# Second product of the MLP: 16 of its 22 K tiles as seven half-block products, with sums of weights made by adding DMAs

## The chip, the cores and the metric

One core of a Trainium2 chip runs the whole program. The metric is the time of one execution on the device, in microseconds; the median of three runs is given, and one more execution was recorded by the hardware profiler. The names of the engines are those of the profile: PE (TensorE, matrix products), PEld (its weight loads), DVE (VectorE), ACT (ScalarE), POOL (GpSimd), SP (SyncE, which here only issues DMAs).

## What is computed

One layer of a decoder: token mixers, a projection, and a gated MLP, all in float32. The part that matters here is the end:

```
h = rmsnorm(x, ln_ffn_g)                          # x: 512 tokens x 1024
a, u = split(h @ w_ffn_in)                        # 1024 -> 2 x 2816
a = causal_dwconv(a, conv_w, conv_b)
x = x + (silu(a) * u) @ w_ffn_out                 # 2816 -> 1024
```

## The kernel before

Everything is cut into tiles of 128: 4 blocks of tokens, 8 tiles of the model's width, 22 tiles of the MLP's width. A product of float32 data is done as three matmuls in the type float32r: an operand x is split into a high half (a cast on ACT, `wh`) and a low half (x minus the high half, on DVE, `wl`), and high x high, high x low and low x high are added up in PSUM (`mm3`). Activations get the same split when they are made.

Weights arrive in units of up to 1 MB on SP's queue (`load`; tile `raw`, four buffers). A unit is used in chunks. For each chunk `split_steps` casts and subtracts (`wh` has four buffers, `wl` three), and a function of the chunk issues the matmuls. The main loop at the end of the program goes over the chunks and asks for the splits of the current one and the next two. PE's instructions stand in program order (`order`); so do POOL's DMAs (`pool`); on ACT and DVE a scheduler sets the order among what is independent.

The first product (`ffn_group`) already uses seven products instead of eight half-block products (the Strassen form with Winograd's order of sums). Sums of activations are made on DVE. Sums of weights are made in place, in the tile `raw`: as soon as a chunk has been split, a DMA from POOL's queue adds another 512 KB block of the weights from HBM onto it (`then`, `accum_op=ALU.add`), and the next chunk that uses the tile splits the sum.

The second product is plain. The gated activations lie in `gT` (22 tiles of 128 x 512 tokens). `fo_split` makes their halves, two tiles ahead. All eight PSUM banks are held through the product: 4 token blocks x 2 halves of the 1024 columns. One chunk is one K tile (128 x 1024 weights): 8 x 3 matmuls of 512 columns, with the activations as the stationary operand and the weights moving. The last three K tiles (`TAIL`) are taken bank by bank, so that a finished bank is added to the residual `x1` on DVE (L794) and stored on SP's queue (L795) while PE works on the next. The residual was put into HBM (`spill`) before the first product and is loaded back when the second begins.

## Time and profile before

| | us |
|---|---|
| median of three runs (803.85 to 804.54) | 803.97 |
| the profiled execution, its own time | 803.51 |
| its span, first to last instruction | 801.7 |
| PE busy in the span | 789.6 |
| DVE busy | 524.2 |
| ACT busy | 371.5 |
| POOL busy | 161.1 |

An execution takes a little longer than its span. PE's busy time is the sum of modelled, overlapping matmuls, so its steps are better read from the starts of matmuls than from their lengths. The granted clock of PE is 0.998 of full speed over the span, which is the upper of its two levels, 2.4 GHz.

### The profile page before, as it was taken

Reading aid. Unit: us, or ns where it says so; the run is one execution under the profiler, and the core shown is the slowest. Engines: PE = TensorE matmul, PEld = TensorE weight load, DVE = VectorE, ACT = ScalarE, POOL = GpSimd, SP = SyncE. Lnnn points to the kernel's source line nnn. Section 1 sums busy time; section 2 is a strip of 40 time slices with the busy share of each in tenths; the row PEclk is TensorE's granted clock in tenths of the full one; section 3 lists DMA queues with packets and bytes.
Section 4 is the critical chain, followed back from the end, with each engine's and each line's share of the span. In section 5 each row is a group of like instructions: output and inputs, shape, how many; then the busy total and the mean of one; then the engine's idle time right before and its main releaser. Section 6 shows DMA issues by size and latency. Waiting matters only on the chain.

```text
span 801.7 us, 11534 instructions
## 1 busy us (share of the span) xinstructions
PE 789.6 (98%) x4550; PEld 693.9 (87%) x4550; DVE 524.2 (65%) x805; ACT 371.5 (46%) x566; POOL 161.1 (20%) x221
## 2 busy tenths in 40 slices
PE   8999999999999999999999999999999999999997
PEld 8888888878878888888888999999999999788886
DVE  5777656764989883546744767867777778623323
ACT  6663333547644542533432755555555665423210
POOL 1510010004767740000010131212222320000000
PEclk9999999999999999999999999999999999999999
DMA  9513132231212113232593399789999995432002
GB/s 326 159 52 105 55 104 75 83 106 53 76 63 72 54 54 103 81 106 83 197 272 105 83 162 204 146 161 185 180 185 184 170 222 181 149 105 74 32 1 106
DMA packets 74888, 98.49 MB, mean 123 GB/s; under 512 B 3644, under 2 KB 60578, under 8 KB 74834
## 3 DMA queue, kind: packets, MB, share of 16 engines
q1 hardware_dynamic: 51490, 74.57, 28.0%
q0 software_dynamic: 23232, 23.07, 19.2%
q8 instruction: 36, 0.59, 0.3%
q14 instruction: 18, 0.15, 0.1%
q10 hardware_dynamic: 112, 0.10, 0.0%
HBM read 93.54 MB, written 4.19 MB: 122 GB/s over the span
## 4 chain that ended last, share of the span: by engine, by line
PE 83%; DVE 7%; DMA 3%; POOL 2%; ACT 2%; issue 2%; SPq 0%; ACTq 0%; POOLq 0%; DVEq 0%
PE ps L84 81%; DMA raw<-in_w_ffn_in_dram 2%; PE ps L107 2%; DVE wl L271 1%; DVE stQ L887 1%; POOL stQ L892 1%; DMA raw<-in_w_in_dram 1%; ACT acth L319 1%; DVE t2a L705 1%; DVE t2a L704 1%; DVE scr L930 0%; DVE gT L707 0%; DVE stK L873 0%; ACT wh L270 0%; ACT t4a L331 0%
## 5 line engine op out<-in xcount | busy, mean ns | idle before, releaser
L271 DVE TENSOR_TENSOR wl<-raw,wh 128x1024 fp32r<-128x1024 f32 (+1 forms) x152 | 186.7, 1230 | 117.3 <-PE ps L84 59.7
L270 ACT CAST wh<-raw 128x1024 fp32r<-128x1024 f32 (+1 forms) x150 | 157.1, 1048 | 208.7 <-PE ps L84 164.1
L84 PE MATMUL ps<-wh,acth 128*128 128x512 f32 (+1 forms) x352 | 131.9, 385 | 0.5 <-DVE wh L268 0.5
L84 PE MATMUL ps<-s,wh 128*128 128x256 f32 x704 | 129.3, 285 | 2.5 <-ACT gT L689 2.5
L84 PE MATMUL ps<-wl,acth 128*128 128x512 f32 (+1 forms) x352 | 130.3, 381 | 0.8 <-DVE wl L271 0.8
L84 PE MATMUL ps<-wh,actl 128*128 128x512 f32 (+1 forms) x352 | 130.3, 381 | 0.0
L84 PEld LDWEIGHTS ps<-s,wh 128*128 128x128 f32 x704 | 110.2, 192 | 2.7 <-ACT gT L689 2.7
L718 POOL DMA_DIRECT2D raw<-in_w_ffn_in_dram x44 | 56.7, 1289 | 254.9 <-DVE wl L271 132.6
L84 PE MATMUL ps<-s,wl 128*128 128x256 f32 x352 | 100.3, 285 | 0.0
L84 PE MATMUL ps<-a,wh 128*128 128x256 f32 x528 | 96.3, 283 | 0.0
L84 PEld LDWEIGHTS ps<-a,wh 128*128 128x128 f32 x528 | 81.8, 190 | 0.1
L84 PE MATMUL ps<-acth,wh 128*128 128x512 f32 x192 | 79.4, 413 | 0.0
L84 PEld LDWEIGHTS ps<-wh,acth 128*128 128x128 f32 x352 | 64.7, 188 | 13.4 <-issue 1.5
L84 PEld LDWEIGHTS ps<-wl,acth 128*128 128x128 f32 x352 | 64.7, 188 | 13.3 <-DVE wl L271 1.4
L84 PEld LDWEIGHTS ps<-wh,actl 128*128 128x128 f32 x352 | 64.7, 188 | 12.8
L84 PE MATMUL ps<-acth,wl 128*128 128x512 f32 x192 | 75.1, 391 | 0.0
L84 PE MATMUL ps<-actl,wh 128*128 128x512 f32 x192 | 74.9, 390 | 0.0
L84 PE MATMUL ps<-a,wl 128*128 128x256 f32 x264 | 74.7, 283 | 0.0
L84 PEld LDWEIGHTS ps<-s,wl 128*128 128x128 f32 x352 | 67.5, 192 | 0.0
L84 PEld LDWEIGHTS ps<-a,wl 128*128 128x128 f32 x264 | 50.1, 190 | 0.0
L892 POOL TENSOR_TENSOR stQ<-stQ,qk 128x128 f32<-128x128 f32 (+2 forms) x80 | 46.3, 605 | 10.4 <-ACT stQ L90 8.7
L84 PEld LDWEIGHTS ps<-acth,wl 128*128 128x128 f32 x192 | 36.0, 188 | 7.9
(233 smaller groups left out, 1229.1 us busy)
## 6 DMA issues: line engine op xcount, KB each, us to landing
raw<-in_w_in_dram SPq DMA_DIRECT2D x22, 1024.0 KB
raw<-in_w_ffn_in_dram POOLq DMA_DIRECT2D x44, 512.0 KB, 6.5
raw<-in_w_ffn_in_dram SPq DMA_DIRECT2D x22, 512.0 KB
raw<-in_w_ffn_out_dram SPq DMA_DIRECT2D x11, 1024.0 KB
b<-in_w_ffn_in_dram SPq DMA_DIRECT2D x11, 512.0 KB
raw<-in_w_branch_b_dram SPq DMA_DIRECT2D x4, 1024.0 KB
raw<-in_w_out_dram SPq DMA_DIRECT2D x4, 1024.0 KB
x<-in_x_dram SPq DMA_DIRECT2D x4, 512.0 KB
```

What stands on the lines that cost most here:

```text
L84: order(nc.tensor.matmul(ps, lhsT, rhs, start=start, stop=stop, skip_group_check=more))
L107: order(nc.tensor.transpose(ps, src, idn))
L270: nc.scalar.copy(h[:, k], src[:, k])
L271: nc.vector.tensor_sub(l[:, k], src[:, k], h[:, k].bitcast(F32))
L319: nc.scalar.mul(hT[0][:, k, tok], ps, g)
L704: nc.vector.scalar_tensor_tensor(t, A[:, c, 1:S + 1], col(1), t, ALU.mult, ALU.add)
L705: nc.vector.scalar_tensor_tensor(t, A[:, c, 0:S], col(0), t, ALU.mult, ALU.add)
L718: pool(nc.gpsimd.dma_start(loaded[u][:, half[a], :], chain[a], accum_op=ALU.add))
L887: nc.vector.tensor_tensor(v[:, :, :, c], Bg[:, hs, :, t], r.broadcast_to([P, 2, P // (per * L), (per - 1 - j) * L]), ALU.subtract)
L892: nc.gpsimd.tensor_tensor(v[:, :, :, c], v[:, :, :, c], qg[:, hs, :, t], ALU.mult)
```

## The change

The first six K tiles of the second product stay plain; when they are done, the eight banks are added into `x1` in SBUF. The other sixteen tiles become two halves of eight K tiles, the tokens two halves of 256, the columns two halves of 512, and the product is done as seven half-block products in the order of `FSEQ`. One of them is 8 K tiles x 2 token blocks x 3 = 48 matmuls of 512 columns, in four chunks of two K tiles. `fo_part` makes the activations' operand of the product that follows, with sums on DVE; `fo_evac` adds each finished product into `x1`, or keeps it in `F["v"]`; a12 goes on adding in the banks of a11, and s4 in those of s1. Three blocks of weights are loaded (2 MB each: for a11, a12 and s4); the weights of the other four products arise in those tiles by sixteen adding DMAs of 512 KB. The last three chunks of a22 are taken bank by bank. Units are fetched two ahead instead of three from the start of the first product on.

The diff, without its empty lines:

```diff
--- before.py
+++ after.py
@@ -249,9 +249,13 @@
         if i not in split and i < len(chunks):
             run(split_steps(i))
 
+    def ahead(i):
+        return 2 if i < 2 or i >= n_o else 3
     def split_steps(i):
         u, sl, shape, _ = chunks[i]
-        for uu in range(u, u + 3 if i > 1 else 2):
+        for uu in range(u, u + ahead(i)):
             load(uu)
         n = shape[0] * shape[1]
         src = sl() if callable(sl) else loaded[u][:, sl[0], sl[1]]
@@ -743,62 +747,157 @@
         groups[g](a)
     n_fi = len(chunks)
 
-    fo_act = []
+    FP, FH = 6, 8
+    fo, fo_act = {}, []
 
     def fo_split(j):
         if j < 2:
             H, L = tmp([P, S], "gh", F32R), tmp([P, S], "gl", F32R)
         else:
             if j == 2:
-                fo_act.extend(act_pair("act"))
-            H, L = (t[:, j % KT, :] for t in fo_act)
+                fo_act.extend(v3(slot(n, F32R), 4) for n in ("foh", "fol"))
+            H, L = (t[:, j - 2, :] for t in fo_act)
         nc.scalar.copy(H, gT(j))
         nc.vector.tensor_sub(L, gT(j), H.bitcast(F32))
         return H, L
 
-    TAIL = 3
-    fo = {}
-    def fo_mm(i, j, b, half, wh, wl, H, L):
-        ps = st["fo"][b][half]
-        t, w = slice(b * P, (b + 1) * P), slice(half * 512, (half + 1) * 512)
-        matmul(ps, H[:, t], wh[:, 0, w], start=j == 0, stop=False)
-        matmul(ps, H[:, t], wl[:, 0, w], start=False, stop=False)
-        matmul(ps, L[:, t], wh[:, 0, w], start=False, stop=j == NF - 1)
-    early = {}
     def fo_ready(j):
-        for jj in range(j + 1):
-            if jj < NF and jj not in early and jj not in fo:
-                early[jj] = fo_split(jj)
+        for jj in range(min(j + 1, FP)):
+            if jj not in fo:
+                fo[jj] = fo_split(jj)
+    def x1q(b, half):
+        return x1(b)[:, half * 512:(half + 1) * 512]
 
     def fo_chunk(j):
         def mm(i):
             if j == 0:
                 st["fo"] = [[bank() for _ in range(2)] for _ in range(NB)]
             fo_ready(j + 2)
-            fo[j] = (i, j) + (split[i], early.pop(j))
-            if j < NF - TAIL:
-                for b in range(NB):
-                    for half in range(2):
-                        fo_mm(i, j, b, half, *split[i], *fo[j][3])
-            elif j == NF - 1:
-                for b in range(NB):
-                    for half in range(2):
-                        for jj in range(NF - TAIL, NF):
-                            ii, _, (wh, wl), (H, L) = fo[jj]
-                            fo_mm(ii, jj, b, half, wh, wl, H, L)
-                        w = slice(half * 512, (half + 1) * 512)
-                        o = tmp([P, 512], "t2a")
-                        nc.vector.tensor_tensor(o, st["fo"][b][half], x1(b)[:, w], ALU.add)
-                        nc.sync.dma_start(out[b * P:(b + 1) * P, w], o)
+            if j >= FP - 4:
+                for c in range(FH // 2 * (j - FP + 4) // 4, FH // 2 * (j - FP + 5) // 4):
+                    fo_part("a11", c)
+            (H, L), (wh, wl) = fo[j], split[i]
+            for b in range(NB):
+                t = slice(b * P, (b + 1) * P)
+                for half in range(2):
+                    ps, w = st["fo"][b][half], slice(half * 512, (half + 1) * 512)
+                    mm3(ps, H[:, t], L[:, t], wh[:, 0, w], wl[:, 0, w], j == 0, j == FP - 1)
+                    if j == FP - 1:
+                        nc.vector.tensor_tensor(x1q(b, half), ps, x1q(b, half), ALU.add)
         return mm
 
-    for j in range(0, NF, 2):
+    for j in range(0, FP, 2):
         u = unit([((ALL, ALL), w_fo.rearrange("(k p) c -> p k c", p=P)[:, j:j + 2, :])], (2, D))
         for c in range(2):
             chunk(u, (slice(c, c + 1), slice(0, D)), (1, D), fo_chunk(j + c))
+    FSEQ = ("a11", "a12", "s1", "s2", "s4", "s3", "a22")
+    fop, F = {}, {}
+    def fo_part(a, c):
+        if a not in fop:
+            fop[a] = [v3(slot(f"fo{a}", F32R), FH) for _ in range(2)]
+        (a11, a21), (a12, a22) = ([gT2(FP + half + 2 * c)[:, :, t] for t in (slice(0, 256), slice(256, S))]
+                                  for half in (0, FH))
+        src = {"a11": a11, "a12": a12, "a22": a22, "s2": a21}.get(a)
+        if src is None:
+            src = tmp([P, 2, 256], f"f{a}")
+            if a == "s1":
+                nc.vector.tensor_sub(src, a21, a22)
+                nc.vector.tensor_sub(a21, a11, src)
+            else:
+                nc.vector.tensor_sub(src, a12 if a == "s4" else a22, a21)
+        h, l = (t[:, 2 * c:2 * c + 2, :] for t in fop[a])
+        nc.scalar.copy(h, src)
+        nc.vector.tensor_sub(l, src, h.bitcast(F32))
+    def fo_evac(a, b):
+        ps = F[a][b]
+        lo, hi = b, 2 + b
+        def put(y):
+            nc.sync.dma_start(out[y[0] * P:(y[0] + 1) * P, y[1] * 512:(y[1] + 1) * 512], x1q(*y))
+        def add(y, z, sub=False):
+            nc.vector.tensor_tensor(x1q(*y), x1q(*y), z, ALU.subtract if sub else ALU.add)
+        if a == "a11":
+            if b == 0:
+                F["v"] = tmp([P, 2, 512], "fv")
+            nc.scalar.copy(F["v"][:, b, :], ps)
+            return
+        v = F["v"][:, b, :]
+        if a == "a12":
+            add((lo, 0), ps)
+            put((lo, 0))
+        elif a == "s1":
+            add((hi, 1), ps)
+        elif a == "s2":
+            nc.vector.tensor_sub(v, ps, v)
+            add((lo, 1), v)
+        elif a == "s4":
+            add((lo, 1), ps)
+            put((lo, 1))
+        elif a == "s3":
+            nc.vector.tensor_add(v, ps, v)
+            add((hi, 1), v)
+            put((hi, 1))
+            add((hi, 0), v, True)
+        else:
+            add((hi, 0), ps)
+            put((hi, 0))
+    def fo_mm(a, c):
+        def mm(i):
+            on = {"a12": "a11", "s4": "s1"}.get(a)
+            if c == 0:
+                F[a] = F[on] if on else [bank() for _ in range(2)]
+            n = FSEQ.index(a) + 1
+            if n < len(FSEQ):
+                fo_part(FSEQ[n], c)
+            nc_ = FH // 2
+            tail = a == FSEQ[-1]
+            todo = [(c, i, b) for b in range(2)]
+            if tail and c:
+                todo = [(cc, i - c + cc, b) for b in range(2) for cc in range(1, nc_)] if c == nc_ - 1 else []
+            for cc, ii, b in todo:
+                (H, L), (wh, wl) = fop[a], split[ii]
+                for j in range(2):
+                    sl = (ALL, 2 * cc + j, slice(b * P, (b + 1) * P))
+                    mm3(F[a][b], H[sl], L[sl], wh[:, j, :], wl[:, j, :], not on and cc + j == 0,
+                        cc == nc_ - 1 and j == 1, bool(on))
+                if cc == nc_ - 1:
+                    fo_evac(a, b)
+        return mm
+    def fo_block():
+        rows = w_fo.rearrange("(k p) c -> p k c", p=P)
+        q = lambda half, i, cols: rows[:, FP + half * FH + i:FP + half * FH + i + 4, 512 * cols:512 * cols + 512]
+        load4 = lambda half, i, cols: unit([((ALL, ALL), q(half, i, cols))], (4, 512))
+        place = {}
+        for a in FSEQ:
+            if a in ("a11", "a12", "s4"):
+                own = [load4(*{"a11": (0, i, 0), "a12": (1, i, 0), "s4": (1, i, 1)}[a]) for i in range(0, FH, 4)]
+            place[a] = {"s1": "a11", "s2": "a11", "a22": "a11", "s3": "s4"}.get(a, a)
+            if place[a] == a:
+                place[a] = own
+            else:
+                place[a] = place[place[a]]
+            for c in range(FH // 2):
+                u, half = place[a][c // 2], slice(2 * (c % 2), 2 * (c % 2) + 2)
+                nxt = {"a11": (0, 1), "s1": (1, 1), "s2": (1, 0), "s4": (0, 1)}.get(a)
+                if nxt:
+                    src = q(nxt[0], c // 2 * 4, nxt[1])[:, half, :]
+                    then[len(chunks)] = lambda u=u, half=half, src=src: pool(
+                        nc.gpsimd.dma_start(loaded[u][:, half, :], src, accum_op=ALU.add))
+                chunk(u, (half, slice(0, 512)), (2, 512), fo_mm(a, c))
+    fo_block()
 
 
     gla = {}
```

On DVE, where the plain tiles of the second product run, `wl` are low halves of weights, `actl` (before) and `foa` low halves of activations, `fs` and `gT` sums of activations. Before:

```order
L271 TENSOR_TENSOR wl_6442<-raw_5795,wh_6441 128x1024
L271 TENSOR_TENSOR wl_6474<-raw_6311,wh_6473 128x1024
L271 TENSOR_TENSOR wl_6510<-raw_6311,wh_6509 128x1024
L756 TENSOR_TENSOR actl_6413<-gT_4691,acth_6411 128x512
L271 TENSOR_TENSOR wl_6542<-raw_6397,wh_6541 128x1024
L756 TENSOR_TENSOR actl_6413<-gT_4691,acth_6411 128x512
L271 TENSOR_TENSOR wl_6572<-raw_6397,wh_6571 128x1024
L756 TENSOR_TENSOR actl_6414<-gT_5156,acth_6412 128x512
```

After:

```order
L275 TENSOR_TENSOR wl_6438<-raw_6309,wh_6437 128x1024
L275 TENSOR_TENSOR wl_6470<-raw_6395,wh_6469 128x1024
L815 TENSOR_TENSOR foa_902_6623<-gT_5153,foa_901_6622 128x512
L815 TENSOR_TENSOR foa_902_6623<-gT_5618,foa_901_6622 128x512 x2
L815 TENSOR_TENSOR foa_902_6623<-gT_5886,foa_901_6622 128x512
L809 TENSOR_TENSOR fs_916_6706<-gT_3967,gT_5153 128x512
L809 TENSOR_TENSOR fs_919_6727<-gT_4688,gT_5618 128x512
L275 TENSOR_TENSOR wl_6510<-raw_6395,wh_6509 128x1024
L810 TENSOR_TENSOR gT_3967<-gT_3967,fs_916_6706 128x2x256
L810 TENSOR_TENSOR gT_4688<-gT_4688,fs_919_6727 128x2x256
L809 TENSOR_TENSOR fs_922_6749<-gT_4688,gT_5618 128x512
L809 TENSOR_TENSOR fs_925_6771<-gT_5153,gT_5886 128x512
```

Between the splits of one tile and the next, where one low half stood, there are now the low halves of a12 and sums for s1, s2 and s4.

On DVE further on, from the third split of a11 (`wl` of the second half of its weights): `fos` are low halves of the sums for the products s1 and s2, `raw_6613` is the unit for a12. After (before, only a split and a low half follow each other by turns here, as in the first of these fences):

```order
L275 TENSOR_TENSOR wl_6616<-raw_6541,wh_6615 128x1024
L815 TENSOR_TENSOR fos_915_6705<-fs_916_6706,fos_914_6704 128x512
L275 TENSOR_TENSOR wl_6639<-raw_6541,wh_6638 128x1024
L815 TENSOR_TENSOR fos_915_6705<-fs_919_6727,fos_914_6704 128x512
L815 TENSOR_TENSOR fos_915_6705<-fs_922_6749,fos_914_6704 128x512
L815 TENSOR_TENSOR fos_915_6705<-fs_925_6771,fos_914_6704 128x512
L275 TENSOR_TENSOR wl_6660<-raw_6613,wh_6659 128x1024
L812 TENSOR_TENSOR fs_954_6948<-gT_5886,gT_5153 128x512
L812 TENSOR_TENSOR fs_959_6975<-gT_5153,gT_3967 128x512
L812 TENSOR_TENSOR fs_962_6996<-gT_5618,gT_4688 128x512
L275 TENSOR_TENSOR wl_6678<-raw_6613,wh_6677 128x1024
```

Just ahead of this piece stand the eight additions of the six plain tiles into `x1c` and `x1d`, which come after the second split of a11.

On POOL, at the end of its queue. Before, these are the last adding DMAs of the first product:

```order
L686 MEMSET conva_6076 128x2x2
L718 DMA raw_5284<-in_w_ffn_in_dram 128x4x256
L718 DMA raw_5516<-in_w_ffn_in_dram 128x4x256
```

After, eight rows follow those, sixteen adding DMAs, in the order a11, s1, s2, s4, with nothing between them:

```order
L897 DMA raw_6467<-in_w_ffn_out_dram 128x2x512 x2
L897 DMA raw_6541<-in_w_ffn_out_dram 128x2x512 x2
L897 DMA raw_6467<-in_w_ffn_out_dram 128x2x512 x2
L897 DMA raw_6541<-in_w_ffn_out_dram 128x2x512 x2
L897 DMA raw_6467<-in_w_ffn_out_dram 128x2x512 x2
L897 DMA raw_6541<-in_w_ffn_out_dram 128x2x512 x2
L897 DMA raw_6698<-in_w_ffn_out_dram 128x2x512 x2
L897 DMA raw_6920<-in_w_ffn_out_dram 128x2x512 x2
```

POOL's queue, which ended with the first product, now reaches to the end of s4.

In SP's queue one load of 512 KB (`b`, near the start of the first product) stands one place earlier, the three units of the plain tiles are followed by the six loads of the seven products, and the eight stores come last.

## Rows read from the trace of the kernel before

**Rows 1.** The page: busy us of each engine (share of the span) x instructions

```profile
PE 789.6 (98%) x4550; PEld 693.9 (87%) x4550; DVE 524.2 (65%) x805; ACT 371.5 (46%) x566; POOL 161.1 (20%) x221
```

**Rows 2.** The chain that ended last: start us, length us, engine, tile, line

```profile
512.87 0.49 issue
513.36 7.03 DMA raw<-in_w_ffn_in_dram
...
688.73 108.90 PE ps L84 x479
797.66 0.69 DVE t2a L794
```

**Rows 3.** Stretches: busy PE, PEld, DVE, ACT, POOL (xcount), clock, DMA share, GB/s

```profile
550.00:600.00 50.00, 50.00 (x419) 50.00 (x419) 37.45 (x45) 27.76 (x34) 11.88 (x12) 1.00 0.88 174
...
720.00:740.00 20.00, 20.00 (x90) 16.58 (x89) 7.31 (x8) 6.30 (x8) 0.00 (x0) 1.00 0.25 85
```

**Rows 4.** Single matmuls of the second product: start us, length us

```profile
676.30 0.39 PE L84 MATMUL ps<-wh,gh 128*128 128x512 f32 x1
...
681.96 0.40 PE L84 MATMUL ps<-wh,gh 128*128 128x512 f32 x1
...
687.54 0.39 PE L84 MATMUL ps<-wh,acth 128*128 128x512 f32 x1
...
769.80 0.39 PE L84 MATMUL ps<-wl,acth 128*128 128x512 f32 x1
...
773.88 0.39 PE L84 MATMUL ps<-wl,acth 128*128 128x512 f32 x1
...
797.23 0.39 PE L84 MATMUL ps<-wh,actl 128*128 128x512 f32 x1
```

**Rows 5.** Waits of PE from 500 us on: us in total, times, longest

```profile
PE ps L84 <- ACT gT L689: 2.5, 1, 2.5
PE ps L84 <- DVE wl L271: 0.8, 1, 0.8
```

**Rows 6.** Groups by line and shape, 680 to 802 us: busy us, mean ns

```profile
L271 DVE TENSOR_TENSOR wl<-raw,wh 128x1024 fp32r<-128x1024 f32 x20 | 24.4, 1224 | 62.8 <-issue 45.9 <-PE ps L84 16.9
L270 ACT CAST wh<-raw 128x1024 fp32r<-128x1024 f32 x18 | 18.9, 1048 | 17.4 <-PE ps L84 17.2
L756 DVE TENSOR_TENSOR actl<-gT,acth 128x512 fp32r<-128x512 f32 x12 | 8.2, 686 | 0.0
L755 ACT CAST acth<-gT 128x512 fp32r<-128x512 f32 x12 | 7.5, 628 | 47.8 <-PE ps L84 47.8
```

**Rows 7.** DVE in order of time, first product

```profile
572.83 0.69 DVE L691 TENSOR_TENSOR v<-ps,v 128x512 f32<-128x512 f32 x1 [0.62 <-PE ps L84]
573.43 1.22 DVE L271 TENSOR_TENSOR wl<-raw,wh 128x1024 fp32r<-128x1024 f32 x1
574.57 0.68 DVE L692 TENSOR_TENSOR gT<-ps,v 128x512 f32<-128x512 f32 x1
```

**Rows 8.** The tile raw from 430 us: POOL's issues, and issue to landing

```profile
L718 POOL DMA_DIRECT2D raw<-in_w_ffn_in_dram x42: 1273/1282/1309, 454.5 to 655.0; - x42
...
DMA to landing us min/median/max: 5.8/6.6/12.4
```

**Rows 9.** DMA, 586 to 588 us (adding only), then 580 to 594

```profile
DMA packets 379, 0.38 MB, mean 189 GB/s; under 512 B 9, under 2 KB 379, under 8 KB 379
...
q0 software_dynamic: 379, 0.38, 122.5%
...
GB/s 202 287 304 383 378 377 386 383 328 202 199 187 202 228 173 181 193 190 196 187 187 187 193 196 190 161 146 143 187 196 193 202 199 252 331 328 392 246 73 26
```

**Rows 10.** The page's DMA queue of POOL: packets, MB, share

```profile
q0 software_dynamic: 23232, 23.07, 19.2%
```

**Rows 11.** POOL in order of time: the last adding DMAs

```profile
646.40 1.28 POOL L718 DMA_DIRECT2D raw<-in_w_ffn_in_dram  x1 [4.72 <-DVE wl L271]
...
655.04 1.29 POOL L718 DMA_DIRECT2D raw<-in_w_ffn_in_dram  x1 [1.26 <-DVE wl L271]
```

## The prediction

> **What bounds the kernel now.** I read the page's head first: TensorE (PE) is busy 789.6 of 801.7 us, DVE 524.2 [rows 1]. The reader is to see there that no other engine comes near. Then the chain that ended last [rows 2]: from 688.73 us on it is one piece of matmuls, 108.90 us long, and behind it only the final addition at 797.66 and the store of its result; the time from that addition's start to the end of the span is 4.0 us. So in the second product of the MLP every matmul that goes away shortens the kernel, unless something else becomes late. Last the stretches [rows 3]: in the second product VectorE (DVE) works 7.3 of 20 us and the DMA engines a quarter of the time; in the first product, which already has the seven-product form with adding DMAs, DVE works 37.5 of 50 us and DMA stands at 0.88, and PE is still full. That stage is my model of what the second product turns into.
>
> **What is removed.** Before, the 22 K tiles take 22 x 24 = 528 matmuls of 512 columns. After, 6 tiles stay as they are (144), and 16 tiles x 512 tokens x 1024 columns become seven products of 48 matmuls (336): 480, so 48 fewer. Their starts go from 676.30 to 797.23, 527 steps [rows 4]. Two gaps are in it: 1.0 us after 687.54, where the next matmul starts at 688.73, 1.19 later instead of 0.23 (0.8 of it is told as a wait for a DVE split, [rows 2, 4, 5]), and some 0.2 near 681. (120.93 - 1.2) / 527 = 0.2272 us for one. 48 x 0.2272 = **10.9 us**, all on the path.
> The TensorE page of the Trainium skill, "TensorE: Matmul & The Clock Gate" (Back-to-back issue gap, and the figure before it), has 215.7 ns between matmuls of 512 columns. By it the gain would be 48 x 0.2157 = 10.4 us. The trace disagrees by 5%, and the sum goes by the trace.
> The pace is not quite constant: in the busiest part, from 681.96 to 687.54, 24 steps take 0.2325 each, late in the stage 18 steps take 0.2267 [rows 4]. If the 336 matmuls beside busier engines and DMA all ran at 0.2325, that would give back 336 x 0.0053 = 1.8 us; if at the average, 0. I take 0.3, since that pace lasted only for those few us.
>
> **What is added on ScalarE and DVE.** The weights now come as 6 + 28 = 34 splits instead of 22. In the seven products a chunk has 12 matmuls, 2.73 us, instead of 24. Costs by row [rows 6]: a DVE split 1.22 us, a 512-column DVE operation 0.69; but one starts before its predecessor has ended: 1.14 after a split, 0.60 after a short operation [rows 7]. Those steps are what counts on a full queue.
> DVE in the seven products: 28 splits x 1.14 = 31.9, 24 low halves of activations x 0.61 = 14.6 (the four of a11 are made earlier), 16 sums of activations x 0.61 = 9.8, 18 additions on the results x 0.61 = 11.0: 67.3 us, against 336 x 0.2272 = 76.3 of PE. Tight, but the order helps: the scheduler has put eleven of the sixteen sums before the end of the six plain tiles. There, from 687.5, are 21.8 us of matmuls (four tiles) for three splits and some seventeen short operations, 13.8 us. Product by product DVE then has, with what the order puts between the splits (four splits are 4.6): a11 13 short operations, 12.5 us; a12 10, 10.7; s1 9, 10.0; s2 6, 8.2; s4 4, 7.0; s3 2, 5.8; each against 10.9. Only a11 is over, by 1.6 us. The low weights have three buffers, so a split can begin two chunks, 5.5 us, before PE needs it and be done some 4 us before; the 1.6 comes out of that. ScalarE has 28 x 1.05 + 24 x 0.63 + 1.3 = 45.8 us. So neither engine holds PE up: **0**, as long as the 4 us of lead last.
> a12 adds onto the banks of a11, so PE must wait until ScalarE has copied the second bank: 0.6 us after its last matmul, and PE comes to it six matmuls, 1.36 us, later. Cover 0.7; lost if a weight cast (1.05) stands in between: 0 to 0.4.
> DVE's four low halves of a12 stand where the last SiLU steps of the first product end; the wait of 0.8 us on DVE there [rows 5] may grow by one short operation. I take 0.2 for these two, and 0.1 for the last three chunks of a22, which PE takes bank by bank: the last split waits for the buffer of a22's first chunk and has twelve matmuls' time, 2.7 us, for 1.2 us and the additions before it.
>
> **What is added on POOL and the DMA engines.** Sixteen adding DMAs of 512 KB. Each waits for the split that reads its tile; the split of the product after next on that tile waits for its landing. Nothing else is left in POOL's queue, and POOL takes 1.28 us each. From the end of a split to POOL's start 0.5 us [rows 2], to landing 6.6 in the median [rows 8], then cast and split 1.05 + 1.22 + 0.1: 9.5 us. From s1 to s2 and from s4 to s3 a tile comes back after four chunks, 10.9 us. 1.4 us remain, and with 3.5 of the lead 4.9.
> What can use that up is rate. From s1 to s4 twelve adding DMAs are issued in a row, one per chunk of 2.73 us. Where nothing but adding DMAs runs in the first product, 189 GB/s move [rows 9]: 0.524 MB in 2.77 us. (Plain loads show 380 GB/s at the start of the last row there.) Twelve of them fall back by 12 x 0.04 = 0.5 us; two result stores and what is left of a 1 MB load, 0.8 MB, add 2.1. Backlog at the last one 2.6 us, below 4.9: **0**. In general the loss is 12 x (T - 2.73) + 2.1 - 4.9 with T us for one, nothing up to T = 2.96.
> Above, a row shows the issue step at 1.27 to 1.31 us in 42 cases beside a DVE that is 75% busy with two-input operations [rows 3, 8]: no sign of waiting. The page "SBUF — State Buffer" (Who interferes with whom) says that DVE with two SBUF inputs and POOL when it reads SBUF lock each other out, and warns that descriptors from POOL starve behind DVE. By that rule each issue could wait out one split; the trace does not show it, and the sum leaves it out.
> Rows are 2 KB now instead of 1 KB. No row has an adding DMA of that shape: between half the packets at the same time each (1.4 us) and the same bytes at worse than the page's share (19.2% of 801.7 us for 23.07 MB, [rows 10], is 3.5 us each if packets did not overlap). I take 2.77, the same bytes.
>
> **What moves.** The result of the six tiles is added into the residual early, eight DVE operations, so the residual must be back from HBM: its loads stand where they stood. Units are fetched two ahead instead of three in the first product: one load of 512 KB moves up by one place in SP's queue near 440 us; 0. The 2.5 us near 520, where PE waited for ScalarE behind a late adding DMA [rows 2, 5], stay: the order there is the same, and the three runs of before lie within 0.7 us, so such a wait does not come and go; 0. The tail is as before: one addition, one store of 256 KB, 4.0 us.
>
> **Sum.** -10.9 + 0.3 + 0.2 + 0.1 = -10.3 us on the profiled execution: 803.51 becomes 793.2. The median of the three runs is 0.46 above that execution, 803.97: **793.6 us**.
>
> **The rivals.**
> Slower pace: PE runs at 0.2325 beside full DVE and DMA: 1.8 instead of 0.3, 795.1. For it the early stretch, against it the rest of the stage.
> Adding DMAs at 3.3 to 3.5 us each: loss 12 x 0.57 - 2.8 = 4.0 to 6.4, shown as PE waiting at the start of s3: 797.6 to 800.0. For it the page's share, against it 189 GB/s in [rows 9], where the share is over 100%, so packets overlap.
> DVE as the bound: if operations on full queues took their whole 1.22 and 0.69, the sum would be 28 x 1.22 + 58 x 0.69 = 74.2 of 76.3, and a11's and a12's excess (13.9 + 11.8 - 21.8 = 3.9, s1 another 0.2) would eat the lead: 2 to 4 us, 795.6 to 797.6.
> Slower: adding DMAs that need a landing each, one after the other. At 5.8 us, the shortest landing [rows 8], the loss is 12 x 3.07 - 2.8 = 34 us: 827. The gain is gone at T = 3.8 and it is slower by over 0.2% from 4.0. Against it: the four issued from 646.40 to 655.04 had the last landed after 12.4 us [rows 8, 11], 21 us for four although the spilled residual and weights went beside them.
>
> **How the numbers follow.** Forecast 0.55, slower pace 0.10, adding DMAs at 3.3 to 3.5 0.17, DVE 0.08, serial adding DMAs 0.07, between them and no change 0.03. The range goes from 792.0 (nothing given back, the 1.0 us gap at 687.54 gone too) to 799.5, which leaves out the slow cases and the end of the second rival, some 0.15. This kernel's runs differ by 0.1%, so 0.2% is about what can be told: faster 0.90, same 0.03, slower 0.07.
>
> **What would show it.** In the profile after: 480 matmuls from about 676 to 786.5; PE's waits still under 2 us in the stage; DVE near nine tenths from a11 to s1; adding DMAs landing in 6 to 9 us. Wrong: PE waiting for ScalarE casts in s3 behind a DMA (rate), for DVE splits in a12 or s1 (DVE), or matmul starts more than 0.23 apart (pace).

## The result, and the profile after

The changed kernel took 793.01 us in the median of four runs (792.34 to 794.23), the kernel before 803.91 beside it: a ratio of 0.9867, 95% interval 0.985 to 0.9884. The forecast was 793.6, the range 792.0 to 799.5. The profiled run took 792.45 us with a span of 790.8, 10.9 less than the span of before.

First the page's head: busy time of each engine, then the DMA queues (packets, MB, share of 16 engines' span). It answers to [rows 1, 10].

```profile
PE 777.5 (98%) x4502; PEld 683.2 (86%) x4502; DVE 565.7 (72%) x863; ACT 392.0 (50%) x592; POOL 179.9 (23%) x237
...
q0 software_dynamic: 27584, 31.46, 25.6%
```

48 matmuls fewer and 12.1 us less of PE's (overlapping) busy time; DVE works 41.5 us more, POOL 18.8 us more, and the queue of the adding DMAs moves 8.39 MB more. All that work came in and the time still fell by almost exactly the matmuls. The chain that ended last (start, length, what; x: instructions in the piece) answers to [rows 2]:

```profile
513.70 7.05 DMA raw<-in_w_ffn_in_dram
...
687.60 1.14 DVE wl L275
688.78 98.00 PE ps L84 x431
786.81 0.69 DVE x1d L826
```

The last piece of matmuls was 108.90 us long and is 98.00, and its start did not move (688.73 before). The wait on a late adding DMA near 513 us, in the first product, is still there. But what came behind it differs between the two profiled runs. Four microseconds from there, before and after (length; busy time and instructions of PE, PEld, DVE, ACT, POOL; granted clock, DMA share, GB/s):

```profile
522.00:526.00 4.00, 3.93 (x20) 3.93 (x21) 3.08 (x5) 2.38 (x4) 1.29 (x1) 0.57 1.22 199
522.00:526.00 4.00, 3.57 (x30) 3.57 (x31) 3.08 (x4) 2.75 (x4) 1.29 (x1) 1.00 1.22 205
```

Before, PE waited 2.54 us and its granted clock then fell; after, it waited 2.71 us and the clock stayed. The 24 matmuls that follow take 4.47 us before and 2.97 after, 1.50 less. It is not tied to the change: in seven of the ten experiments, which all start from the changed kernel, the clock falls there too. Where the pieces of the second product start, by PE's matmuls in time (start, length):

```profile
675.48 0.39 PE L84 MATMUL ps<-wh,gh 128*128 128x512 f32 x1
...
687.60 0.39 PE L84 MATMUL ps<-wh,foh 128*128 128x512 f32 x1
688.78 0.50 PE L84 MATMUL ps<-wl,foh 128*128 128x512 f32 x1 [0.80 <-DVE wl L275]
...
710.45 0.39 PE L84 MATMUL ps<-wh,foa 128*128 128x512 f32 x1
...
786.38 0.39 PE L84 MATMUL ps<-wh,foa 128*128 128x512 f32 x1
```

`foa` at 710.45 is the first matmul of a11, 786.38 the last of a22: 335 steps in 75.93 us, 0.2267 each, without one gap. The six plain tiles before it take 34.97 us and hold the only waits, 0.8 on the DVE split (as before) and 0.6 on a DVE step of the convolution. All of PE's waits from 400 us on (total, times, longest) are these three:

```profile
PE ps L84 <- ACT gT L693: 2.7, 1, 2.7
PE ps L84 <- DVE wl L275: 0.8, 1, 0.8
PE ps L84 <- DVE conva L702: 0.6, 1, 0.6
```

What stands beside the seven products, stretch by stretch (length; busy time and instructions of PE, PEld, DVE, ACT, POOL; granted clock, DMA share, GB/s):

```profile
709.00:720.00 11.00, 11.00 (x51) 9.09 (x50) 10.88 (x15) 6.31 (x8) 2.39 (x2) 1.00 0.78 134
720.00:731.00 11.00, 11.00 (x50) 9.13 (x49) 10.55 (x15) 8.73 (x13) 1.19 (x1) 1.00 0.68 200
731.00:742.00 11.00, 11.00 (x51) 9.09 (x50) 8.90 (x12) 5.87 (x8) 4.88 (x5) 1.00 1.08 213
742.00:753.00 11.00, 11.00 (x50) 9.13 (x49) 8.62 (x11) 5.28 (x5) 4.89 (x5) 1.00 1.12 201
753.00:764.00 11.00, 11.00 (x50) 9.09 (x50) 7.55 (x9) 4.23 (x4) 3.38 (x3) 1.00 1.12 202
764.00:775.00 11.00, 11.00 (x50) 9.13 (x49) 6.31 (x7) 4.23 (x4) 0.00 (x0) 1.00 0.15 53
```

PE is full in each of them. DVE stands at 10.88 and 10.55 of 11 in the first two and falls from there, as the prediction's product-by-product list had it. DMA is saturated from 731 to 764. There ScalarE does wait for it, at the casts of s3 (start, length, what it waited for):

```profile
757.58 1.05 ACT L274 CAST wh<-raw 128x1024 fp32r<-128x1024 f32 x1 [2.35 <-DMA raw<-in_w_ffn_out_dram]
760.11 1.06 ACT L274 CAST wh<-raw 128x1024 fp32r<-128x1024 f32 x1 [1.48 <-DMA raw<-in_w_ffn_out_dram]
762.66 1.06 ACT L274 CAST wh<-raw 128x1024 fp32r<-128x1024 f32 x1 [1.49 <-DMA raw<-in_w_ffn_out_dram]
765.20 1.06 ACT L274 CAST wh<-raw 128x1024 fp32r<-128x1024 f32 x1 [1.49 <-DMA raw<-in_w_ffn_out_dram]
```

The casts come 2.54 us apart: that is the adding DMA's T, read where the queue alone sets it. It is below 2.73, so the lead eats the wait and PE never sees it. From 740 to 760 us, where only adding DMAs run, the queue shows the same (0.524 MB at 199 GB/s is 2.63 us), and the sums' issue and landing, beside [rows 8], are these (POOL's duration min/median/max in ns; landing in us):

```profile
L897 POOL DMA_DIRECT2D raw<-in_w_ffn_out_dram x16: 1188/1197/1207, 702.6 to 758.3; - x16
...
DMA to landing us min/median/max: 5.5/7.3/8.1
```

### The profile page after: what moved, and what is told of

It reads as the page before. It is cut to its first block, busy times and chain, and to the rows that moved or that the text cites. A ratio compares the mean times of both kernels' runs of the same rounds, so it can differ in the third digit from the quotient of the medians.

```text
span 790.8 us, 11572 instructions
## 1 busy us (share of the span) xinstructions
PE 777.5 (98%) x4502; PEld 683.2 (86%) x4502; DVE 565.7 (72%) x863; ACT 392.0 (50%) x592; POOL 179.9 (23%) x237
## 4 chain that ended last, share of the span: by engine, by line
PE 84%; DVE 8%; DMA 3%; POOL 2%; ACT 2%; issue 1%; SPq 0%; ACTq 0%; POOLq 0%; DVEq 0%
PE ps L84 81%; DMA raw<-in_w_ffn_in_dram 3%; PE ps L107 2%; DVE wl L275 2%; DVE stQ L986 1%; DVE scr L1029 1%; DMA raw<-in_w_in_dram 1%; POOL stQ L991 1%; ACT acth L323 1%; DVE t2a L709 1%; DVE t2a L708 1%; DVE gT L711 0%; DVE stK L972 0%; ACT t4a L335 0%; POOL g L920 0%
## 5 line engine op out<-in xcount | busy, mean ns | idle before, releaser
L274 ACT CAST wh<-raw 128x1024 fp32r<-128x1024 f32 (+1 forms) x162 | 170.1, 1051 | 227.2 <-PE ps L84 164.5
L275 DVE TENSOR_TENSOR wl<-raw,wh 128x1024 fp32r<-128x1024 f32 (+1 forms) x164 | 201.6, 1230 | 69.5 <-PE ps L84 53.8
L84 PE MATMUL ps<-wh,acth 128*128 128x512 f32 (+1 forms) x192 | 69.7, 382 | 0.9 <-DVE wh L272 0.9
L84 PE MATMUL ps<-wh,actl 128*128 128x512 f32 (+1 forms) x192 | 68.0, 374 | 0.0
L84 PE MATMUL ps<-wl,acth 128*128 128x512 f32 (+1 forms) x192 | 67.9, 373 | 0.0
L991 POOL TENSOR_TENSOR stQ<-stQ,qk 128x128 f32<-128x128 f32 (+2 forms) x80 | 46.3, 606 | 10.3 <-ACT stQ L90 9.5
L84 PEld LDWEIGHTS ps<-acth,wh 128*128 128x128 f32 x192 | 36.1, 188 | 7.1 <-ACT wh L274 0.4
L84 PEld LDWEIGHTS ps<-actl,wh 128*128 128x128 f32 x192 | 36.1, 188 | 6.4
L84 PEld LDWEIGHTS ps<-wh,acth 128*128 128x128 f32 x192 | 34.7, 188 | 7.7 <-ACT acth L323 1.2
```

The lines of the kernel that those rows point to most:

```text
L84: order(nc.tensor.matmul(ps, lhsT, rhs, start=start, stop=stop, skip_group_check=more))
L274: nc.scalar.copy(h[:, k], src[:, k])
L275: nc.vector.tensor_sub(l[:, k], src[:, k], h[:, k].bitcast(F32))
L991: nc.gpsimd.tensor_tensor(v[:, :, :, c], v[:, :, :, c], qg[:, hs, :, t], ALU.mult)
```

## The experiments

Every experiment changes the kernel after, and is compared with it and with the kernel before, timed beside it. Line names: `wh` is the cast of weights on ACT, `wl` the split on DVE, `raw` the weight tile.

**Are the adding DMAs free?** None is issued, so s1, s2, s3 and a22 multiply weights without their sums:

```diff
-                if nxt:
+                if nxt and False:
```

> The changed kernel without its sixteen adding DMAs in the second product (so the products s1, s2, s3 and a22 multiply unsummed weights; that part of the computation is wrong). Theory (the 480 matmuls set the end, the adding DMAs are wholly hidden): no gain beyond what runs differ by, 792 to 793.5. Rival (matmuls or splits run slower beside the adding DMAs): the steps between matmuls shrink from 0.227 and the time falls by 0.5 to 2 us.

Measured: 791.76 us (791.1 to 793.63), ratio 0.9853 (0.9835 to 0.9871). The interval overlaps that of the change (0.985 to 0.9884), so sixteen DMAs of 512 KB cost nothing that can be told. The median lies 1.25 us lower, as the rival of the expectation had it, but not for the rival's reason: the 335 steps of the seven products take 75.94 us in this trace (709.88 to 785.82), 0.2267 each, as in the changed kernel. The rivals that put 4 us or more on them fall.

**Does the fetch distance of the first product matter?** Three units ahead again there:

```diff
-        return 2 if i < 2 or i >= n_o else 3
+        return 2 if i < 2 or i >= n_fi else 3
```

> The changed kernel with units fetched three ahead again in the first product, two ahead only in the second. Theory (the fetch distance in the first product hides behind other chunks): same time as the changed kernel, 792 to 794, and the same 2.5 to 2.7 us gap of PE near 520 us. Rival (the shorter distance costs or gains in the first product): a difference of 0.5 to 2.5 us there.

Measured: 793.44 us (791.01 to 795.0), ratio 0.9867. No effect; the wait for ACT near 520 us stays too (3.2 us here).

**Is the matmul the price?** The 48 matmuls of a12 are issued twice, with the same splits and DMAs, so that PE has 528 as before:

```diff
-                    mm3(F[a][b], H[sl], L[sl], wh[:, j, :], wl[:, j, :], not on and cc + j == 0,
-                        cc == nc_ - 1 and j == 1, bool(on))
+                    for k in range(2 if a == "a12" else 1):
+                        mm3(F[a][b], H[sl], L[sl], wh[:, j, :], wl[:, j, :], not on and cc + j == 0,
+                            cc == nc_ - 1 and j == 1 and k == (a == "a12"), bool(on))
```

> The changed kernel with the 48 matmuls of the product a12 issued twice (the result is wrong by one more a12): 528 matmuls of 512 columns in the second product, as many as the kernel before, with all the rest of the change. Theory (the matmul count alone sets the end): 48 x 0.2272 = 10.9 us more than the changed kernel, 803.5 to 804.5, the time of the kernel before. Rival (some of the gain or loss lies in the other edits): off from that by 1 us or more.

Measured: 804.59 us (803.05 to 805.12, ten runs), ratio 1.0005 (0.9994 to 1.0015): the kernel before to within its noise, 11.6 above the change where 10.9 were expected. In its trace the seven products take 86.81 us from first matmul to last (711.50 to 798.31) where they took 75.93, 10.88 more for the 48 steps; the other 0.7 is within what the runs differ by. All that the change added is in this kernel, and none of it shows.

**How much more may the queue carry?** Twelve more adding DMAs of 256 KB onto a tile that nothing reads:

```diff
...
+                        if a != "a11":
+                            if not extra:
+                                extra.extend(tmp([P, 2, 512], "dm") for _ in range(2))
+                                for t in extra:
+                                    nc.vector.memset(t, 0.0)
+                            pool(nc.gpsimd.dma_start(extra[c // 2][:, c % 2, :], src[:, 0, :], accum_op=ALU.add))
...
```

> The changed kernel with twelve further adding DMAs of 256 KB, one behind each of those of s1, s2 and s4, onto a tile that nobody reads: half as many bytes again. Theory (the adding DMAs are a queue with a rate; one of 512 KB takes 2.6 to 2.8 us when they run back to back, and PE waits when the queue falls back by more than 4.9 us): T becomes 3.9 to 4.2, loss 12 x (T - 2.73) - 2.8 = 11 to 15 us, 804 to 808, with PE waiting at s3 behind ScalarE casts that wait for a DMA. Rival (the landing is latency, not rate): within 1 us of 793.

Measured: 802.23 us (801.32 to 803.52, eight runs), ratio 0.9985 (0.9974 to 0.9996), 9.2 above the change where 11 to 15 were expected: nearly the whole gain. ScalarE's casts in s3 now come 3.83 us apart, each behind its DMA:

```profile
767.75 1.04 ACT L274 CAST wh<-raw 128x1024 fp32r<-128x1024 f32 x1 [13.18 <-DMA raw<-in_w_ffn_out_dram]
771.59 1.05 ACT L274 CAST wh<-raw 128x1024 fp32r<-128x1024 f32 x1 [2.79 <-DMA raw<-in_w_ffn_out_dram]
775.40 1.05 ACT L274 CAST wh<-raw 128x1024 fp32r<-128x1024 f32 x1 [2.77 <-DMA raw<-in_w_ffn_out_dram]
```

The stretch from 764 to 775 us, full above, reads here:

```profile
764.00:775.00 11.00, 6.05 (x17) 4.21 (x16) 3.05 (x3) 2.09 (x2) 2.14 (x2) 0.69 1.13 205
```

The place is the forecast one, but the granted clock of 0.69 was not in the formula. The next run shows what it is worth.

**And a quarter more?** As above with 128 KB each:

```diff
...
+                            pool(nc.gpsimd.dma_start(extra[c // 2][0:64, c % 2, :], src[0:64, 0, :], accum_op=ALU.add))
...
```

> Twelve further adding DMAs of 128 KB each (64 partitions of 512 columns) onto a tile that nothing reads, one beside each of the sums that the chunks of s1 and s2 order ahead; nothing of the computation is left out. Each tile's sums then move 640 KB where the changed kernel moves 512 KB. At the 2.55 to 2.63 us that 512 KB took in the changed kernel's trace this is 3.2 to 3.3 us per tile. Theory of the one queue (formula of the prediction, 12 x (T - 2.73) + 2.1 - 4.9): a loss of 2.8 to 4.0 us, so 795.8 to 797.0 us, with ScalarE's last casts of s3 waiting for the queue and TensorE for them. Rival, that the queue's slack is larger than the formula has it (the first sums are ordered earlier than it reckons, and TensorE's last product can be late without loss): within 1 us of the changed kernel, 792 to 794. Rival, that every further byte is paid for, with no slack at all: 12 x 0.65 us = 7.8 us, about 801.

Measured: 800.92 us (799.04 to 802.23, eight runs), ratio 0.9963 (0.995 to 0.9977), 7.9 above the change where 2.8 to 4.0 were expected. Two things made the difference. The queue was slower than expected for a part of the way: 182 GB/s in the mean from 740 to 760 us, so 640 KB take 3.60 us, not 3.2. It was 173 GB/s from 742 to 754 us and 202 from 758 to 770, with the same mix of whole and small DMAs, and ScalarE's casts of s3 come 3.19 us apart; what slowed the queue in the first of these stretches is not shown.

```profile
767.89 1.04 ACT L274 CAST wh<-raw 128x1024 fp32r<-128x1024 f32 x1 [12.58 <-DMA raw<-in_w_ffn_out_dram]
771.08 1.04 ACT L274 CAST wh<-raw 128x1024 fp32r<-128x1024 f32 x1 [2.15 <-DMA raw<-in_w_ffn_out_dram]
```

And PE's matmuls in time, where it stood in s3, show what a pause costs:

```profile
764.71 0.39 PE L84 MATMUL ps<-wh,fos 128*128 128x512 f32 x1
768.99 0.80 PE L84 MATMUL ps<-wh,fos 128*128 128x512 f32 x1 [3.89 <-ACT wh L274]
770.25 0.80 PE L84 MATMUL ps<-wl,fos 128*128 128x512 f32 x1 [0.46 <-DVE wl L275]
770.84 1.05 PE L84 MATMUL ps<-wh,fos 128*128 128x512 f32 x2
771.69 0.63 PE L84 MATMUL ps<-wl,fos 128*128 128x512 f32 x1
...
775.52 0.62 PE L84 MATMUL ps<-wh,fos 128*128 128x512 f32 x2
```

From 764.71 to 775.52 are fifteen steps, 3.40 us at the pace of 0.2267; they took 10.81. Of the 7.41 us lost, 4.35 are the two waits in brackets; most of the other 3.06 are matmuls that start 0.43 apart instead of 0.23, until 774.7, at a granted clock of 0.50, the lower of the two levels (1.2 GHz). That place holds the whole difference: the last matmul is 7.52 us later than in the changed kernel (793.90 against 786.38). In the run with 256 KB the same count from 763.97 to 773.96 gives eleven steps, 7.50 us lost, 4.95 of waits and 2.55 of the rest, mostly clock. So a late cast there is paid once in waiting and then by half as much again and more.

The time itself, 7.9 us above the change, is what the rival without any slack named (7.8). Its mechanism does not hold: the waits here are 4.35 us, and by it the run with 256 KB, where T grew from 2.54 to 3.83 us, would have lost 12 x 1.29 = 15.5 us, where 9.2 were lost.

**Do short rows cost?** Each adding DMA in two of 256 columns, so rows of 1 KB as in the first product, and 32 issues:

```diff
-                    then[len(chunks)] = lambda u=u, half=half, src=src: pool(
-                        nc.gpsimd.dma_start(loaded[u][:, half, :], src, accum_op=ALU.add))
+                    def add(u=u, half=half, src=src):
+                        for w in (slice(0, 256), slice(256, 512)):
+                            pool(nc.gpsimd.dma_start(loaded[u][:, half, w], src[:, :, w], accum_op=ALU.add))
```

> Each adding DMA of the change is split in two of 256 columns, so that its rows are 1 KB as in the kernel before, and GpSimd issues 32 where it issued 16; nothing of the computation is left out. Theory of the one queue: the rate falls back from about 199 to 206 GB/s to the 189 GB/s of the kernel before, so 512 KB take 2.77 us, still under the 2.96 us at which the formula's loss begins: no change, 792 to 794 us; GpSimd's issues of 1.2 to 1.3 us, two per tile, 2.6 us, fit beside 2.8 us per tile. Rival, that the short rows or the doubled issues cost more than that: ScalarE's casts in s3 wait for the queue, TensorE waits for them, and the time is 795 or more.

Measured: 792.6 us (792.32 to 793.92), ratio 0.9864 (0.985 to 0.9879): no change. Queues and rate from 740 to 758 us:

```profile
DMA packets 3508, 3.39 MB, mean 188 GB/s; under 512 B 206, under 2 KB 3507, under 8 KB 3507
...
q0 software_dynamic: 3507, 3.38, 120.9%
```

188 GB/s with rows of 1 KB, 199 with 2 KB, and the 189 of [rows 9] from another stage: the rate of these sums hangs little on the row's length. At 188 GB/s T is 2.79 us, still under 2.96.

**How much room has DVE?** One more 512-column subtraction per chunk, onto a tile that nothing reads:

```diff
...
+            nc.vector.tensor_sub(dm[0][:, 0, :], dm[0][:, 1, :], split[i][1][:, 0, :].bitcast(F32))
```

> The changed kernel with one more 512-column operation on DVE for each of the 28 chunks, after the chunk's split, into a tile that nobody reads. Theory (DVE is some nine tenths busy from a11 to s1 and has 4 us of lead): a11, a12 and s1 then take 15.1, 13.3 and 12.6 us of DVE against 10.9 of PE; 8 us over, 4 of them lead: loss about 4 us, 797, PE waiting for splits in a12 and s1. Rival (DVE has ample room): within 1 us of 793.

Measured: 793.43 us (792.52 to 794.33, two runs), ratio 0.987 (0.985 to 0.989). The expected 4 us did not come, though DVE is now full in four of the six stretches, three of which are:

```profile
720.00:731.00 11.00, 11.00 (x51) 9.09 (x50) 11.00 (x16) 7.33 (x11) 0.92 (x1) 1.00 0.70 215
731.00:742.00 11.00, 11.00 (x50) 9.13 (x49) 11.00 (x15) 4.70 (x6) 5.07 (x5) 1.00 0.99 196
...
753.00:764.00 11.00, 11.00 (x50) 9.13 (x49) 11.00 (x16) 5.26 (x6) 4.29 (x4) 1.00 1.03 176
```

The expectation added each product's local excess to the lead. But the order is not fixed: the scheduler put what is needed later behind the urgent splits. The last five sums for s4 and s3 (`fs`, L812) stood at 717 to 731 us and now stand at 729 to 762, the low halves for a22 went from 745 to 748 us to 766 to 775. The first line is from the changed kernel, the second from this run:

```profile
717.29 1.89 DVE L812 TENSOR_TENSOR fs<-gT,gT 128x512 f32<-128x512 f32 x3
...
761.33 0.68 DVE L812 TENSOR_TENSOR fs<-gT,gT 128x512 f32<-128x512 f32 x1
```

So the excess spread over the stage, and the stage's total counts, as the next run bears out.

**Twice that:** two extra subtractions per chunk:

```diff
...
+            for k in range(2):
+                nc.vector.tensor_sub(dm[0][:, 0, :], dm[0][:, 1, :], split[i][1][:, k, :].bitcast(F32))
```

> The changed kernel with two more 512-column operations on DVE for each of the 28 chunks (one more cost nothing: DVE then had no idle time from 711 to 775 us, and what was not urgent went behind the splits). Theory (what binds on DVE is the sum over the stage, and with one more it is just full): the second costs all its 28 x 0.61 = 17 us but for a few, 804 to 810, PE waiting for splits. Rival (what binds is the lead of the splits alone, which the order can keep): within 2 us of 793.

Measured: 809.29 us (806.03 to 810.52, six runs), ratio 1.0062 (1.0045 to 1.008). PE's waits in the stage and one of its stretches:

```profile
PE ps L84 <- DVE wl L275: 11.2, 15, 2.3
```

```profile
753.00:764.00 11.00, 9.46 (x39) 6.83 (x38) 11.00 (x17) 3.31 (x5) 3.58 (x3) 1.00 0.92 146
```

Now the total is over PE's, and DVE is the bound. The room is thus more than one and less than two operations per chunk, as the totals say: in the changed kernel's trace DVE is busy for 78.5 of the 99.3 us from 687.5 us to its last addition at 786.81, so 20.8 are free. One more operation per chunk is 28 x 0.6 = 16.8 us and fits; two are 33.6, 12.8 too much, and 16.3 were lost. Fifteen waits, none over 2.3 us, left the clock at 1.00 here.

**What is next, if PE needed less?** The third of each three matmuls (low activations x high weights) is left out in the seven products, 112 fewer, with all other work kept:

```diff
-                    mm3(F[a][b], H[sl], L[sl], wh[:, j, :], wl[:, j, :], not on and cc + j == 0,
-                        cc == nc_ - 1 and j == 1, bool(on))
+                    matmul(F[a][b], H[sl], wh[:, j, :], not on and cc + j == 0, False, bool(on))
+                    matmul(F[a][b], H[sl], wl[:, j, :], False, cc == nc_ - 1 and j == 1, bool(on))
```

> The changed kernel without the third matmul (low half of the activations x high half of the weights) in the seven products, 112 fewer (the result loses that small part). By PE alone 112 x 0.2272 = 25.4 us less, 767.6. Theory (the adding DMAs and DVE come next): twelve adding DMAs at 2.6 us from about 722 on end near 757, then cast, split, the last chunk of s3 and the four of a22, 7.3 us: end of PE at 768 to 770 instead of 761; DVE, 58 us of work after 710, ends about there too. So 775 to 779, with PE waiting in s3 or before. Rival (both have ample room): 768.

Measured: 784.56 us (two runs, 784.55 and 784.56), ratio 0.9754 (0.9734 to 0.9773). Of the 25.4 us that PE alone would give, 8.5 came, less than expected. Two of the stretches and PE's waits:

```profile
731.00:742.00 11.00, 9.14 (x37) 6.34 (x36) 7.16 (x8) 7.60 (x11) 3.74 (x4) 1.00 1.12 213
...
753.00:764.00 11.00, 8.69 (x28) 6.19 (x29) 8.70 (x11) 6.67 (x8) 0.00 (x0) 0.84 0.75 162
```

```profile
PE ps L84 <- DVE wl L275: 9.1, 9, 3.9
PE ps L84 <- ACT wh L274: 1.3, 2, 1.0
```

Both covers are thin. The queue is saturated in the first of these stretches, and in the second the clock falls as well. DVE is named in most of PE's waits, but it is busy for only 7.16 and 8.70 of 11 us there: from 700 us on its splits wait 10.0 us for casts, and ScalarE's casts 17.2 us for adding DMAs. DVE itself is full from 762 to 772 us, where the longest of PE's waits falls (3.9 us). So PE meets the queue first and DVE second. Of the missing 16.9 us these waits are 9.6, the 10.4 shown less the 0.8 at 688 us that the changed kernel has too; how the rest divides was not separated.

**The wait at 688 us.** GpSimd instead of DVE makes the low halves of the weights of plain tiles 2 and 3:

```diff
-            nc.vector.tensor_sub(l[:, k], src[:, k], h[:, k].bitcast(F32))
+            low = nc.gpsimd if i in (n_fi + 2, n_fi + 3) else nc.vector
+            low.tensor_tensor(l[:, k], src[:, k], h[:, k].bitcast(F32), ALU.subtract)
```

> The changed kernel with the low halves of the weights of the third and fourth plain tile made on POOL, which idles there, instead of DVE, where they stand behind the last SiLU steps; PE waits 0.8 to 1.0 us for the third tile's. Theory (that wait is DVE's order): the gap near 688 us goes, 0.8 to 1.0 us less than the changed kernel, about 792. Rival (POOL takes longer than DVE is late, or slows DVE): the gap stays or grows by a microsecond or more.

Measured: 794.02 us (791.84 to 795.82), ratio 0.987 (0.9849 to 0.9891): no gain. The wait at 688 is gone, and PE waits 2.4 us for DVE's convolution instead. The two GpSimd operations, and what DVE did beside them:

```profile
675.34 3.22 POOL L276 TENSOR_TENSOR wl<-raw,wh 128x1024 fp32r<-128x1024 f32 x1 [20.28 <-PE ps L84]
683.63 2.65 POOL L276 TENSOR_TENSOR wl<-raw,wh 128x1024 fp32r<-128x1024 f32 x1 [5.07 <-ACT t2a L707]
```

```profile
676.23 2.89 DVE L710 SCALAR_TENSOR_TENSOR t2a<-conva,prm,t2a 128x512 f32<-128x512 f32 x1
...
682.64 0.74 DVE L710 SCALAR_TENSOR_TENSOR t2a<-conva,prm,t2a 128x512 f32<-128x512 f32 x1
683.30 3.54 DVE L709 SCALAR_TENSOR_TENSOR t2a<-conva,prm,t2a 128x512 f32<-128x512 f32 x2
```

The same DVE operation takes 0.74 us alone and 2.89 while GpSimd reads SBUF: DVE stood for most of GpSimd's operation. The Trainium skill, page "SBUF — State Buffer", section "Who interferes with whom", states this: a DVE instruction with two SBUF inputs and a GpSimd instruction that reads SBUF exclude each other. These rows agree. What the split saved on DVE was paid back there.

## Why the prediction was right, step by step

- **The removed matmuls, -10.9 us.** Right. From the second product's first matmul to its last the stage took 120.93 us before [rows 4] and 110.90 after (675.48 to 786.38), 10.03 less, and it began 0.82 us earlier: its last matmul moved from 797.23 to 786.38, by 10.85. The 0.82 is luck of the two profiled runs: the clock fell near 522 us in the one before and not in the one after, which is worth 1.50. So the stage itself gave 10.03, close to the forecast's net 10.3; that the profiled runs differ by more is not the change's doing. Issuing 48 of them again gave the kernel before back.
- **Pace, +0.3.** Too careful. In the seven products the step is 0.2267 with DVE at 96 to 99% beside it at first and DMA above its full share later. The 0.2325 of [rows 4] belongs to the plain tiles early in the stage: there it is still to be seen, some 0.233 from 682.01 to 687.60 (24 steps in 5.59 us). A busy DVE or a busy queue alone does not bring it; what does stays open.
- **Bank copy and the wait at 688, +0.2.** Wrong in place, small in size. The wait at 688 stayed at 0.8, and no wait for the copies of a11 stands in the trace. What is new is a wait of 0.6 on a DVE step of the convolution near 681, where only a gap of some 0.2 had stood. It stands in some of the experiments' traces and not in others: the runs without adding DMAs, with short rows and with the old fetch distance have none.
- **DVE, 0.** Right in result, with 10.88 and 10.55 of 11 where 12.5 and 10.7 per product of 10.9 were forecast. The working was partly wrong: excess product by product is not what eats the lead, since the scheduler moves what is not urgent. Its 67.3 us also leave out the eight additions of the plain tiles, which stand at 706.20 to 711.34 us, on both sides of a11's start. The run with one more operation per chunk should have lost by that working, and did not; the rival "DVE as the bound" rested on the same idea.
- **Adding DMAs, 0.** Right. T is 2.54 to 2.63 us where 2.77 was taken. The formula placed the loss correctly (casts in s3) and had its size nearly right, 10.4 against 9.2 at T = 3.83 and 7.6 against 7.9 at T = 3.60, but not for its reasons, so by luck: it counts twelve DMAs up to the last cast of s3, and the wait that decides comes at the first cast of s3, with nine ordered. With 9 instead of 12 it gives 9 x 0.87 + 2.1 - 4.9 = 5.0 us for T = 3.60 and 9 x 1.10 - 2.8 = 7.1 for T = 3.83; the waits measured there were 4.35 and 4.95, and in the second run 1.26 more up to 782 us. The rest of the loss was mostly the clock, which no term held. The rival "3.3 to 3.5 us each" would by nine DMAs come to 2.3 to 4.1 us of waiting, and to 3.5 to 7.0 if the clock added half to seven tenths of that as it did here: about its own 4.0 to 6.4. No run had such a T. The rival that each needs a landing of its own fell with the casts 2.54 us apart, beside landings of 5.5 to 8.1.
- **Descriptor issue, left out.** Right: 1188 to 1207 ns in all sixteen, three of them beside a DVE that is 96 to 99% busy (712.78, 714.72 and 728.78 us), the others beside 69 to 81%.
- **The wait near 520 and the tail, no change.** Right: 2.7 us for 2.5; from the last addition's start to the end of the span 4.0 us, as before. But the prediction's reason, that such a wait does not come and go, left out the clock behind it, which does: 1.50 us that the runs before and after may each have or not.

## What to carry to other kernels

Where one engine is full and the chain of waits is one long piece of its work, the count of removed instructions times their step from that stage is the gain, and the question is only whether the covers hold; judge them by totals over the stage against what may be reordered, not slice by slice. A queue whose item takes less time than the consumer's step costs nothing, and a slower one (here 3.6 and 3.8 us against a step of 2.73) can cost most of the gain, since its lateness adds up item by item. Price a pause of a full TensorE above its own length: here 4 us of waiting cost 7. And where two profiles are compared, take the stage that was changed by itself: a fall of the clock elsewhere, here 1.50 us, can be larger than what is looked for.

## What the runs showed of the hardware

- After 3.89 us of waiting TensorE ran at its lower clock level for some 5.7 us (matmuls 0.43 us apart), and for some 4.5 us after a wait of 4.49. Fifteen waits of up to 2.3 us, in the run with two more DVE operations per chunk, left the granted clock at 1.00 until the last matmuls.
- The same wait can cost the clock in one run and not in the next. Near 520 us PE waits 2.4 to 3.2 us in all twelve traces; in eight of them the granted clock then fell, as low as 0.50, and in four, the changed kernel's among them, it stayed at 1.00. Nor does the length of one wait decide: in the run with two matmuls instead of three the clock fell (0.53 from 757 to 760 us) behind waits of only 1.00 and 0.77 us.
- DMAs that add to SBUF moved 182 to 206 GB/s however they were cut (128 KB, 256 KB or 512 KB, rows of 1 or 2 KB). The lowest mean, 182, was with small ones over 64 partitions mixed with whole ones, but in that run 12 us at 173 GB/s and 12 at 202 had the same mix.
- A GpSimd operation of 2.65 to 3.22 us that reads SBUF held up DVE's two-input operations for some 2.1 us of it (0.74 us became 2.89; two in a row, 1.40 us alone, became 3.54).
